# A trunk layer on one core: its SwiGLU products by Strassen's scheme, the down projection in a second pass

## The chip, the core and the metric

The kernel runs on one core of a Trainium2 chip. The core has a matrix engine (TensorE, PE in the profile), a vector engine (DVE), a scalar engine (ACT), GpSimd (POOL) and a sync engine (SP) whose queue issues the DMAs. Matrix products end in PSUM, eight banks of 512 float32 columns; everything else lies in SBUF or in DRAM. The metric is the device time of one execution in microseconds.

## The reference

One decoder layer over 1024 tokens of width 1024: three mixing branches, their gated merge, an output projection with residual, and a SwiGLU feed-forward part with its own residual. What matters here is the end:

```python
merged = sum_b sigmoid(gate_b) * (y_b @ w_branch[l, b])
x = x + merged @ w_out[l]
h2 = _rmsnorm(x, g_ffn[l])
x = x + (jax.nn.silu(h2 @ w_ffn_gate[l]) * (h2 @ w_ffn_up[l])) @ w_ffn_down[l]
```

`w_out` is 1024 x 1024, `w_ffn_gate` and `w_ffn_up` 1024 x 2816, `w_ffn_down` 2816 x 1024; all is float32.

## The kernel before

All dense products run transposed: the weights are the stationary operand (128 x 128), the activations [channel, token] the moving one, 512 tokens at a time. Each float32 operand is split into a high and a low part, and a product is three passes, hi\*hi, hi\*lo and lo\*hi, which `mm3` (L839) issues. So one 128 x 128 weight tile against 512 tokens is three matmuls. A split is a copy to `hi` on ACT and a subtraction to `lo` on DVE (`load_split`, L830, for weights that SP loads 512 KB at a time).

The program has four stages. The branches (0 to 793 us) and the merge (`merge_lane`, 793 to 924 us, which leaves the merged activations split in `mgh` and `mgl`) come first. Then the output projection (L889 to L908, 924 to 1014 us): eight strips of 128 output channels; each loads x and its strip of `wout`, runs 8 x 3 x 2 matmuls over both halves of the tokens, adds the result to x in `acc[j]` on DVE, splits it straight into `h2h`/`h2l` with the norm's gain, and lets ACT square it and POOL sum the squares.

The SwiGLU stage (1014 us to the end) takes the 22 strips of 128 hidden channels in blocks of 3, 3, 3, 3, 3, 2, 2, 1, 2 (`BLOCKS`). For one strip `up_lane` (L920) runs 48 gate and 48 up matmuls, all on operands that are resident in SBUF. The norm's row factor `rbc` is multiplied onto the products afterwards (L942, L944), so the first products wait for no factor. Then come the SiLU, the product of the two and its split into `ah`/`al`. `down_lane` (L949) lets a block's activations meet the same block's rows of `wfd`: eight output strips, two banks each, with one DVE addition onto `acc` per bank (L962). A planner (`Lanes`) puts the PE work of these lanes in an order by estimated times, so that one block's down products run beside the next block's up products; the framework's scheduler then orders the other engines' instructions.

Of the kernel before, what the change touches and what calls it, by code (L numbers as in the profile page):

```python
# [19 lines left out]
P = 128  # L20
S = 1024
# [7 lines left out]
BLOCKS = (3, 3, 3, 3, 3, 2, 2, 1, 2)  # L29
WARM = 7  # L30
# ns between a lane's work on the tensor engine and its next, which waits for the other engines
# [45 lines left out]
def trunk(tc, xT, memT, wT, wmkv, wmq0, wmq1, wgv, wfox, a2, par, cst, wbr, wout, wfg, wfu, wfd, outT):  # L77
# [26 lines left out]
    def rsqrt_(out, x, n, inv):  # L104
        """out = (x * inv + eps) ** -0.5 for a few columns"""
# [3 lines left out]
    def row_factors(ssqs, bank, rcol, rb, dg):  # L109
        """squares [d part, tokens], to be summed -> rcol [token, tile], rb [any partition, tokens]"""  # L110
# [16 lines left out]
    # ------------------------------------------------------------------ phase A: projections and branches  # L127
# [31 lines left out]
    def gate_lane(js):  # L159
        """branch gates, transposed; they go where the other lanes wait"""  # L160
# [29 lines left out]
    def strip_lane(src, evac):  # L190
        """one transposed strip of 128 columns"""
# [15 lines left out]
    def mem_group(src, evac):  # L207
        """token-major, 256 columns of both tiles of memory tokens; src [4][P][512]"""
# [15 lines left out]
    def group_lane(src, n, nm, evac, gate=None):  # L224
        """token-major: out[token, n] for nm tiles of tokens; src [4][P][2 * n]"""
# [14 lines left out]
    def split_evac(ps, g, hi, lo):  # L240
        """hi + lo = ps * g (g per partition)"""
# [3 lines left out]
    def head_norm(src, junk, ss):  # L245
        """sums of squares of the 128 columns of each head"""
# [3 lines left out]
    # ---- start: x and the memory tokens  # L250
# [795 lines left out]
```

## Time and profile before

| | |
|---|---|
| measured, median of 3 | 1742.22 us (1742.14 to 1742.38) |
| the profiled execution | 1741.5 us, its span from the first to the last instruction |
| PE busy | 1728.5 us, 99% of the span |
| DVE, ACT, POOL busy | 781.8, 503.4, 122.2 us |
| matmuls | 8807, of which 384 in the output projection and 3168 in the SwiGLU stage |
| granted TensorE clock | 1.00 of the 2.4 GHz level nearly throughout, mean 0.998 |

The profile records one execution. "Busy" is the time in which an engine ran instructions. The chain of waits follows the last instruction back, at each step to what released it. A timeline lists instructions by start; several of one kind in a row are merged as "x2". The profile gives no other time of its execution than the span; the measured median lies 0.7 us above it.

### The profile page before, as it was taken

To read this page: it belongs to the slowest core of one execution; us is meant where nothing else is said; L and a number is where in the kernel's file an instruction comes from. 1 tells how busy PE (TensorE), PEld (TensorE's weight loads), DVE (VectorE), ACT (ScalarE), POOL (GpSimd) and SP (SyncE) were. 2 spreads that over 40 slices of the span, in tenths; PEclk is the share of its full clock that TensorE was granted. 3 is DMA by queue.
4 is the path that set the end of the run, shared out by engine and by line. 5 is a ranking of instruction groups with operands and counts; after the bars stand their busy time and mean duration, and the time that the engine had idled before them with its cause. 6 is when DMAs were issued, how large, how long until landed. Compare 5 with 4: busy or idle time off the path is not lost.

```text
span 1741.5 us, 21268 instructions
## 1 busy us (share of the span) xinstructions
PE 1728.5 (99%) x8807; PEld 1467.4 (84%) x8807; DVE 781.8 (45%) x1268; ACT 503.4 (29%) x859; POOL 122.2 (7%) x94
## 2 busy tenths in 40 slices
PE   8999999999999999999999999999999999999999
PEld 6789988879789999988888878888888888888887
DVE  8435554352436555544474343333433343334435
ACT  6334553232224444433122232121211212121110
POOL 2000000000001000000352210000000000000000
PEclk9999999999999999999999999999999999999999
DMA  6341221111222121117653131110211111111002
GB/s 228 129 129 55 67 74 50 61 61 49 68 88 70 57 73 45 67 64 243 193 191 112 37 111 49 43 55 33 63 47 52 49 49 48 45 52 48 35 13 97
DMA packets 55985, 135.01 MB, mean 78 GB/s; under 512 B 5440, under 2 KB 20304, under 8 KB 55888
## 3 DMA queue, kind: packets, MB, share of 16 engines
q1 hardware_dynamic: 55888, 133.65, 23.5%
q8 instruction: 69, 1.13, 0.3%
q14 instruction: 28, 0.23, 0.0%
HBM read 110.49 MB, written 23.13 MB: 77 GB/s over the span
## 4 chain that ended last, share of the span: by engine, by line
PE 95%; DVE 2%; ACT 1%; DMA 1%; issue 0%; POOL 0%; SPq 0%; DVEq 0%
PE ps L841 18%; PE ps L843 18%; PE ps L845 18%; PE pt L155 5%; PE pt L156 4%; PE pt L157 4%; PE pm L234 4%; PE pm L236 4%; PE pm L235 4%; PE pm L197 2%; PE pm L201 2%; PE pm L199 2%; PE at L789 1%; PE o L801 1%; PE o L802 1%; PE at L762 0%
## 5 line engine op out<-in xcount | busy, mean ns | idle before, releaser
L841 PE MATMUL ps<-h2h,hi 128*128 128x512 f32 x704 | 217.2, 390 | 0.0
L843 PE MATMUL ps<-h2l,hi 128*128 128x512 f32 x704 | 216.9, 389 | 0.0
L845 PE MATMUL ps<-h2h,lo 128*128 128x512 f32 x704 | 216.8, 389 | 0.0
L835 ACT CAST hi<-raw 128x1024 fp32r<-128x1024 f32 x76 | 80.0, 1053 | 415.1 <-PE ps L843 383.7
L234 PE MATMUL pm<-whi,hh 128*128 128x384 f32 (+2 forms) x512 | 162.2, 317 | 0.0
L236 PE MATMUL pm<-whi,hl 128*128 128x384 f32 (+2 forms) x512 | 158.9, 310 | 0.0
L235 PE MATMUL pm<-wlo,hh 128*128 128x384 f32 (+2 forms) x512 | 158.8, 310 | 0.0
L845 PEld LDWEIGHTS ps<-h2h,lo 128*128 128x128 f32 x704 | 132.1, 188 | 27.9 <-DVE lo L836 0.4
L841 PEld LDWEIGHTS ps<-h2h,hi 128*128 128x128 f32 x704 | 132.1, 188 | 27.8 <-ACT hi L835 0.4
L843 PEld LDWEIGHTS ps<-h2l,hi 128*128 128x128 f32 x704 | 132.1, 188 | 27.6
L962 DVE TENSOR_TENSOR acc<-acc,ps 128x512 f32<-128x512 f32 x144 | 92.2, 684 | 120.0 <-PE ps L845 120.0
L155 PE MATMUL pt<-hh,whi 128*128 128x512 f32 x352 | 141.8, 403 | 0.0
L156 PE MATMUL pt<-hl,whi 128*128 128x512 f32 x352 | 137.8, 391 | 0.0
L157 PE MATMUL pt<-hh,wlo 128*128 128x512 f32 x352 | 137.7, 391 | 0.0
L843 PE MATMUL ps<-al,dh 128*128 128x512 f32 x352 | 108.7, 389 | 0.0
L841 PE MATMUL ps<-ah,dh 128*128 128x512 f32 x352 | 108.7, 389 | 0.0
L845 PE MATMUL ps<-ah,dl 128*128 128x512 f32 x352 | 108.7, 389 | 0.0
L836 DVE TENSOR_TENSOR lo<-raw,hi 128x1024 fp32r<-128x1024 f32 x76 | 99.0, 1304 | 18.7 <-ACT hi L835 18.4
L944 DVE TENSOR_TENSOR up<-ps,rbc 128x512 f32<-128x512 f32 x44 | 28.4, 686 | 166.5 <-PE ps L845 166.5
L234 PEld LDWEIGHTS pm<-whi,hh 128*128 128x128 f32 x512 | 96.3, 188 | 2.6
L235 PEld LDWEIGHTS pm<-wlo,hh 128*128 128x128 f32 x512 | 96.4, 188 | 2.5
L236 PEld LDWEIGHTS pm<-whi,hl 128*128 128x128 f32 x512 | 96.2, 188 | 0.0
(283 smaller groups left out, 2884.6 us busy)
## 6 DMA issues: line engine op xcount, KB each, us to landing
tg<-tg_d SPq DMA_DIRECT2D x24, 512.0 KB, 4.3
raw<-in_wT SPq DMA_DIRECT2D x22, 512.0 KB, 4.1
tg_d<-gz SPq DMA_DIRECT2D x22, 512.0 KB, 2.9
raw<-in_wfg SPq DMA_DIRECT2D x22, 512.0 KB, 3.5
raw<-in_wfd SPq DMA_DIRECT2D x22, 512.0 KB, 3.6
raw<-in_wfu SPq DMA_DIRECT2D x22, 512.0 KB, 3.5
raw<-in_wfox SPq DMA_DIRECT2D x16, 384.0 KB, 3.1
raw<-y_d SPq DMA_DIRECT2D x12, 512.0 KB, 4.6
```

The source lines that it names most:

```text
L155: nc.tensor.matmul(ps, hi[:, ks], hh[k][:, sl], start=k == 0, stop=False)
L156: nc.tensor.matmul(ps, hi[:, ks], hl[k][:, sl], start=False, stop=False)
L157: nc.tensor.matmul(ps, lo[:, ks], hh[k][:, sl], start=False, stop=k == KT - 1)
L234: nc.tensor.matmul(ps[:, :n], hh[k][:, ms], hi, start=k == 0, stop=False)
L235: nc.tensor.matmul(ps[:, :n], hh[k][:, ms], lo, start=False, stop=False)
L236: nc.tensor.matmul(ps[:, :n], hl[k][:, ms], hi, start=False, stop=k == KT - 1)
L835: nc.scalar.copy(hi, raw)
L836: nc.vector.tensor_tensor(lo, raw, hi.bitcast(F32), ALU.subtract)
L841: nc.tensor.matmul(ps, hi, a, start=first, stop=False)
L843: nc.tensor.matmul(ps, hi, b, start=False, stop=False)
L845: nc.tensor.matmul(ps, lo, a, start=False, stop=last)
L962: nc.vector.tensor_tensor(acc[j][:, s], acc[j][:, s], ps, ALU.add)
```

## The change

The SwiGLU products become Strassen products of the Winograd form. For a pair of hidden strips, the weights are a 2 x 2 block matrix (two strips by two halves of 512 channels) and the activations too (two halves of 512 channels by two halves of 512 tokens). Seven half-size products (`SEQ`) stand for eight. Four of the seven stationary operands are sums of weight blocks, which DVE computes for every pair (`weights`); four of the seven moving operands (T1 to T4) are sums of activation blocks. The sums of the products are formed in PSUM, by accumulating several products onto one of three banks `a`, `b`, `c`, and reading a bank out in between.

The down projection is done the same way, but its inner dimension is now eleven pairs, so it runs as a second pass: `gate_up(p)` writes the seven forms of the activations to `act_d[p]` in DRAM and the sums of the down weights to `sum_d[p]`; `down` takes them back in four blocks of 3, 3, 3 and 2 pairs (`DOWN`). The residual x waits in DRAM (`x_d`) meanwhile.

The output projection is run by halves of the tokens, so that the first half's norm factor is known early. The normed activations now carry their factor before they are split (`normed`, `hop`), instead of having it multiplied onto the products. Everything before the merge's end stays, but for the pool of the merge's weights, which now lies in a stack that is closed after the merge; the tiles of the later stages take its place.

```diff
-BLOCKS = (3, 3, 3, 3, 3, 2, 2, 1, 2)
+NP = NF // 2
+DOWN = (3, 3, 3, 2)
...
+    w4 = lambda: ws.tile([P, S], F32, tag="w4", bufs=5, name="w4")
+    h4 = lambda: ws.tile([P, S], F32R, tag="h4", bufs=3, name="h4")
+    l4 = lambda: ws.tile([P, S], F32R, tag="l4", bufs=3, name="l4")
...
+    def out_half(h):
...
+        for j in range(KT):
+            x1[j][h] = x = cell("x1")
+            nc.sync.dma_start(x, xT[j][:, sl])
+            raw = w4()
+            nc.sync.dma_start(raw, wout[j])
+            hi, lo = split(h4(), l4(), raw)
+            ps = bank8()
...
+            nc.vector.tensor_tensor(x, x, ps, ALU.add)
+            nc.sync.dma_start(x_d[j][h], x)
+            sq = ws.tile([P, 512], F32, tag="h2", bufs=2, name="sq") if j else ssq
+            nc.scalar.activation(sq, x, AF.Square)
+            if j:
+                nc.vector.tensor_tensor(ssq, ssq, sq, ALU.add)
+            yield ssq
...
+    SEQ = (("b", "A11", "B11"), ("a", "A12", "B21"), ("b", "S2", "T2"), ("c", "S1", "T1"), ("b", "S3", "T3"),
+           ("c", "S4", "B22"), ("b", "A22", "T4"))
+
+    def products(A, B, nk, reads):
+
+        banks = {}
+        for i, (bk, an, bn) in enumerate(SEQ):
+            first = bk not in banks
+            if first:
+                banks[bk] = bank8()
+            ps = banks[bk]
+            for k in range(nk):
+                (ah, al), (bh, bl) = A(an, k), B(bn, k)
+                mm3([ps], ah, al, [(bh, bl)], first and k == 0, k == nk - 1, not first)
+            reads[i](ps)
+            yield
...
+        def keep(t, i, l):
+            def read(ps):
+                t[i][l] = cell("t")
+                nc.scalar.copy(t[i][l], ps)
+            return read
+
+        def plus(t, i, l, then):
+            def read(ps):
+                add(t[i][l], ps, t[i][l])
+                then(i, l)
+            return read
...
+        reads = lambda t, then, last: [keep(t, 0, 0), plus(t, 0, 0, then), keep(t, 0, 1), keep(t, 1, 1),
+                                       plus(t, 1, 1, then), plus(t, 0, 1, then), last]
...
+        sub(t1, b12, b11)
+        sub(t2, b22, t1)
+        sub(t3, b22, b12)
+        sub(t4, b21, t2)
+        for i, t in enumerate((b11, b21, t2, t1, t3, b22, t4)):
+            nc.sync.dma_start(act_d[p][i], t)
+        a11, a12, a22, a21 = d = [cell("d") for i in range(4)]
+        for o in range(4):
+            nc.sync.dma_start(d[o].rearrange("p (j c) -> p j c", c=P), wfd[:, p, :, o, :].rearrange("j p c -> p j c"))
...
+    for k in range(4):
+        (b11, b12), (b21, b22) = x1[k], x1[k + 4]
+        normed(k, 1)
+        normed(k + 4, 1)
+        t2 = w4()[:, :512]
+        sub(b11, b12, b11)
+        sub(t2, b22, b11)
+        hops["T2", k] = hop(hp2, "hb", 20, t2)
+        sub(b21, b21, t2)
+    for k in range(4):
+        hops["T1", k] = hop(hp2, "hb", 20, x1[k][0])
...
+    def down(p0, n, last):
+        ops = {}
+        for i in range(0, 7, 2):
+            for q in range(n):
+                w = min(2, 7 - i)
+                raw = w4()
+                nc.sync.dma_start(raw[:, :w * 512].rearrange("p (o c) -> p o c", c=512),
+                                  act_d[p0 + q][i:i + w].rearrange("o p c -> p o c"))
+                for o in range(w):
+                    t = (hp1, "ha", 8) if i == 0 else (hp2, "hb", 20)
+                    ops[ORDER[i + o], q] = hop(*t, raw[:, o * 512:(o + 1) * 512])
...
+            def into(j, h, done):
+                def read(ps):
+                    t = acc[j][h]
+                    add(t, ps, t)
```

`cell` is a pool of 16 tiles of 128 x 512; it holds the merge's sums, then x, then all of `gate_up`'s results in turn, then `acc`.

Three places show how the instructions stand. The first is ACT where the merge ends. `mgh` is the high part of the merged activations, by strips; the copies to `hi` and to `h_8327` are the first splits of `wout`. Before:

```order
L835 CAST hi<-raw 128x1024
L882 ACTIVATE mgh_7326<-acc_7315 128x512 x2
L882 ACTIVATE mgh_7327<-acc_7316 128x512 x2
L835 CAST hi<-raw 128x1024
L882 ACTIVATE mgh_7328<-acc_7317 128x512 x2
```

and after:

```order
L885 ACTIVATE mgh_7334<-acc 128x512 x2
L885 ACTIVATE mgh_7335<-acc 128x512 x2
L885 ACTIVATE mgh_7336<-acc 128x512
L903 CAST h_8327<-w_8325 128x1024
L885 ACTIVATE mgh_7336<-acc 128x512
L903 CAST h_8363<-w_8361 128x1024
```

The first strip's split stood three strips of the merge ahead; it now stands behind the first half of the last one. Its load waits for one of the merge's last three matmuls, since its tile lies where the merge's weights lay.

The second place is DVE where the output projection ends and the SwiGLU stage begins. Before, with the last two strips' additions and splits of x (`acc`, `h2l`), then the down weights' low part `dl` and the factor (`rc`, `diag`):

```order
L903 TENSOR_TENSOR acc_7316<-acc_7316,ps 128x512 x2
L836 TENSOR_TENSOR lo<-raw,hi 128x1024
L243 SCALAR_TENSOR_TENSOR h2l_8286<-acc_7316,pr,h2h_8278 128x512 x2
L903 TENSOR_TENSOR acc_7317<-acc_7317,ps 128x512 x2
L243 SCALAR_TENSOR_TENSOR h2l_8287<-acc_7317,pr,h2h_8279 128x512 x2
L935 TENSOR_TENSOR dl<-raw,dh 128x1024 x2
L106 TENSOR_SCALAR rc_8815<-ps 128x8
```

After, the last of a row of 30 instructions that stand between the second half's factor and the first operand of T1 (`x_8791`, `x_8473` and so on are blocks of x, `w_9098` and the like the sums T2, `hbl` the low parts):

```order
L995 TENSOR_TENSOR x_8791<-x_8943,x_8791 128x512
L995 TENSOR_TENSOR x_8473<-x_8473,w_9098 128x512
L904 TENSOR_TENSOR hbl<-w_9098,hbh 128x512
L995 TENSOR_TENSOR x_8511<-x_8511,w_9108 128x512
L904 TENSOR_TENSOR hbl<-w_9108,hbh 128x512
L995 TENSOR_TENSOR x_8549<-x_8549,w_9118 128x512
L904 TENSOR_TENSOR hbl<-w_9118,hbh 128x512
L995 TENSOR_TENSOR x_8587<-x_8587,w_9128 128x512
L904 TENSOR_TENSOR hbl<-w_9128,hbh 128x512
L904 TENSOR_TENSOR hbl<-x_8323,hbh 128x512
```

The 30 are 8 normed multiplications, 16 subtractions, one split of weights and five low parts. PE's S2\*T2 of the first gate pair accumulates onto bank `b`, which ACT must first copy out; the copy goes into the cell of `x_8323`, so it waits for the last row shown.

The third place is DVE where the first pass ends and the second begins. Before, down products of one block stood among the up work of the next:

```order
L962 TENSOR_TENSOR acc_7315<-acc_7315,ps 128x512 x2
L962 TENSOR_TENSOR acc_7316<-acc_7316,ps 128x512 x2
L935 TENSOR_TENSOR dl<-raw,dh 128x1024 x2
L962 TENSOR_TENSOR acc_7317<-acc_7317,ps 128x512 x2
L935 TENSOR_TENSOR dl<-raw,dh 128x1024
```

After, from the last product of the last pair (L1050) to the first addition of the down projection:

```order
L1050 TENSOR_TENSOR t<-ps,t 128x512
L904 TENSOR_TENSOR l_12373<-w_12359,h_12372 128x768
L995 TENSOR_TENSOR T<-t 128x512
L904 TENSOR_TENSOR l_12377<-w_12360,h_12376 128x768
L904 TENSOR_TENSOR l_12383<-w_12380,h_12382 128x384
L995 TENSOR_TENSOR T<-t,T 128x512
L995 TENSOR_TENSOR T<-t 128x512
L904 TENSOR_TENSOR l_12478<-w_12467,h_12477 128x768
L995 TENSOR_TENSOR T<-t,T 128x512
L904 TENSOR_TENSOR l_12492<-w_12489,h_12491 128x384
L994 TENSOR_TENSOR d<-d 128x512
L994 TENSOR_TENSOR acc<-ps,acc 128x512
```

The third product of the first down group needs that addition, since it uses the same bank. `d` are the last pair's down weights, whose loads stand on SP behind the writes of the T tiles above, and the loads of `acc` stand behind those.

## Rows read from the trace of the kernel before

**Rows 1.** The page: busy time by engine (part 1), the chain that ended last (part 4).

```profile
PE 1728.5 (99%) x8807; PEld 1467.4 (84%) x8807; DVE 781.8 (45%) x1268; ACT 503.4 (29%) x859; POOL 122.2 (7%) x94
...
PE 95%; DVE 2%; ACT 1%; DMA 1%; issue 0%; POOL 0%; SPq 0%; DVEq 0%
```

**Rows 2.** Busy time by window: us, instructions, granted clock (PEclk), DMA share, GB/s.

```profile
20.00:25.00 5.00, 4.60 (x13) 3.65 (x14) 5.00 (x4) 2.37 (x4) 2.47 (x1) 0.66 0.65 240
885.00:920.00 35.00, 35.00 (x156) 29.01 (x155) 26.36 (x29) 10.76 (x15) 18.60 (x13) 1.00 0.71 227
924.00:1014.00 90.00, 90.00 (x388) 72.14 (x387) 31.90 (x41) 24.05 (x30) 20.84 (x8) 1.00 0.18 59
1200.00:1300.00 100.00, 100.00 (x443) 82.77 (x442) 36.61 (x51) 16.59 (x21) 0.00 (x0) 1.00 0.15 48
```

**Rows 3.** Timeline of PE in the last strip: start, duration, instruction.

```profile
1734.99 0.39 PE L843 MATMUL ps<-al,dh 128*128 128x512 f32 x1
...
1737.26 0.39 PE L845 MATMUL ps<-ah,dl 128*128 128x512 f32 x1
```

**Rows 4.** Timeline of PE at the end of the output projection.

```profile
1012.36 0.63 PE L845 MATMUL ps<-mgh,lo 128*128 128x512 f32 x2
...
1013.76 0.63 PE L845 MATMUL ps<-mgh,lo 128*128 128x512 f32 x2
```

**Rows 5.** Groups by line and shape, 900 to 1741 us: busy us, mean ns, idle before.

```profile
L835 ACT CAST hi<-raw 128x1024 fp32r<-128x1024 f32 x52 | 54.8, 1054 | 342.0 <-PE ps L843 333.2 <-DMA raw<-in_wfg 5.7 <-DMA raw<-in_wfu 2.9
...
L947 DVE TENSOR_TENSOR al<-up,ah 128x512 fp32r<-128x512 f32 x44 | 28.5, 688 | 1.8
...
L946 ACT CAST ah<-up 128x512 fp32r<-128x512 f32 x44 | 26.9, 622 | 67.5 <-DVE up L945 67.5
...
L123 PE MATMUL ps<-diag,ones 128*128 128x512 f32 x4 | 2.0, 618 | 0.6 <-DVE diag L118 0.6
L114 PE MATMUL ps<-ones,ssq 128*128 128x1 f32 x16 | 1.9, 251 | 0.0
...
L943 ACT ACT_TABLE_LOAD x1 | 1.3, 1283 | 0.0
```

**Rows 6.** Timeline of DVE in the output projection.

```profile
1002.99 1.28 DVE L903 TENSOR_TENSOR acc<-acc,ps 128x512 f32<-128x512 f32 x2 [7.46 <-PE ps L845]
1004.19 1.22 DVE L836 TENSOR_TENSOR lo<-raw,hi 128x1024 fp32r<-128x1024 f32 x1
1005.33 1.41 DVE L243 SCALAR_TENSOR_TENSOR h2l<-acc,pr,h2h 128x512 fp32r<-128x512 f32 x2
```

**Rows 7.** DMA issues: KB each, median us to landing.

```profile
raw<-in_wout SPq DMA_DIRECT2D x8, 512.0 KB, 3.5
...
raw<-in_wgv SPq DMA_DIRECT2D x8, 256.0 KB, 2.7
...
y_d<-y SPq DMA_DIRECT2D x32, 128.0 KB, 2.9
```

**Rows 8.** Timeline where the merge ends: wait and its releaser in brackets.

```profile
913.53 1.05 ACT L835 CAST hi<-raw 128x1024 fp32r<-128x1024 f32 x1 [1.02 <-PE ps L843]
...
924.17 0.61 PE L845 MATMUL ps<-hi,lo 128*128 128x512 f32 x2
...
924.62 0.63 PE L841 MATMUL ps<-mgh,hi 128*128 128x512 f32 x2
...
928.96 0.63 ACT L882 ACTIVATE mgh<-acc 128x512 fp32r<-128x512 f32 x1 [1.59 <-POOL acc L880]
```

**Rows 9.** Timeline of PE around an early idle time.

```profile
20.40 0.50 PE L156 MATMUL pt<-hl,w 128*128 128x512 f32 x1 [2.03 <-DVE hl L243]
...
24.09 0.45 PE L156 MATMUL pm<-hl,w 128*128 128x512 f32 x1
```

More of the change, by code (lines that the diff above doesn't have):

```diff
@@ L854, in trunk @@
     ap_ = pool(root, "acc")
-    acc = [ap_.tile([P, S], F32, name=f"acc{k}") for k in range(KT)]
+    cell = lambda name: ap_.tile([P, 512], F32, tag="cell", bufs=16, name=name)
+    acc = [[cell("acc") for h in range(2)] for k in range(KT)]
     BM = ExitStack()
@@ L966, in ffn_lane @@
-    def ffn_lane():
-        lanes.add(factor_lane(), 0)
-        yield lambda: 0 if pools else None
-        f = 0
-        for b, nb in enumerate(BLOCKS):
-            dw, act = [], []
-            for i in range(nb):
-                yield from up_lane(pools[0], f, dw, act)
-                f += 1
-            lanes.add(down_lane(b, dw, act), 0 if b < len(BLOCKS) - 2 else 2 + b)
-    BM.close()
-    pools = [pool(root, "ffn")]
-    lanes.add(ffn_lane(), 1)
-    lanes.run()
+    ws = pool(root, "wstage2", side="right")
@@ new lines, in half_factors @@
+    def half_factors(h, ssq):
+        rcol = cp.tile([P, 4], F32, tag="rcol", bufs=2, name="rcol")
+        dg = ws.tile([P, 512], F32, tag="h2", bufs=2, name="dg")
+        ps = bank8()
+        for t in range(4):
+            nc.tensor.matmul(ps[:, t:t + 1], ssq[:, t * P:(t + 1) * P], ones[:, 0:1], start=True, stop=True)
+        rsqrt_(rcol, ps[:, :4], 4, 1.0 / D)
+        nc.vector.tensor_tensor(dg.rearrange("p (t c) -> p t c", c=P), ident.unsqueeze(1).broadcast_to([P, 4, P]),
+                                rcol.unsqueeze(2).broadcast_to([P, 4, P]), ALU.mult)
+        yield
+        ps = bank8()
+        nc.tensor.matmul(ps, ones, dg, start=True, stop=True)
+        nc.scalar.copy(rbc[:, H2[h]], ps)
+        yield
@@ new lines, in normed, with hop @@
+    def normed(k, h):
+        x = x1[k][h]
+        nc.vector.scalar_tensor_tensor(x, x, pr[:, C_GFFN + k:C_GFFN + k + 1], rbc[:, H2[h]], ALU.mult, ALU.mult)
+        return x
+    def hop(pl, tag, n, src):
+        return split(pl.tile([P, 512], F32R, tag=tag + "h", bufs=n, name=tag + "h"),
+                     pl.tile([P, 512], F32R, tag=tag + "l", bufs=n, name=tag + "l"), src)
+    halves = [out_half(h) for h in range(2)]
+    for ssq in halves[0]:
+        pass
+    fac = half_factors(0, ssq)
@@ new lines, in trunk @@
+    for j, ssq in enumerate(halves[1]):
+        if j in (0, 1):
+            next(fac)
+        if j == 1:
+            for k in range(KT):
+                hops["B11" if k < 4 else "B21", k % 4] = hop(hp1, "ha", 8, normed(k, 0))
+    fac = half_factors(1, ssq)
+    SEQ = (("b", "A11", "B11"), ("a", "A12", "B21"), ("b", "S2", "T2"), ("c", "S1", "T1"), ("b", "S3", "T3"),
[11 more added lines that the diff above has]
+            reads[i](ps)
+            yield
@@ new lines, in trunk @@
+    run = gate_up(0)
+    next(run)
+    next(fac)
+    next(run)
+    next(run)
+    next(fac)
+    for k in range(4):
[9 more added lines that the diff above has]
+        hops["T1", k] = hop(hp2, "hb", 20, x1[k][0])
+    for k in range(4):
+        sub(x1[k][1], x1[k + 4][1], x1[k][1])
+        hops["T3", k] = hop(hp2, "hb", 20, x1[k][1])
@@ L982, in trunk @@
+    p0 = 0
+    for n in DOWN:
+        down(p0, n, p0 + n == NP)
+        p0 += n
     pe.__exit__(None, None, None)
```

217 lines of the change are left out of this document (134 added, 83 removed).

## The prediction

> **What bounds the kernel now.** I read the page's busy times first: PE is busy for 1728.5 of 1741.5 us, and the chain that ended last lies on PE for 95% [rows 1]. So the time is the number of matmuls times their pitch, and any idle time of PE adds to it. Next the windows: in the SwiGLU stage 443 matmuls start per 100 us, 0.226 us each, at a granted clock of 1.00, while DVE is busy for 37% and ACT for 17% of the time and the DMA engines for 15% [rows 2]. All engines but PE have room. Last the timelines, for what one matmul costs in each form: ten matmuls that follow one another on one bank in the last strip take 2.27 us, 0.227 each [rows 3], as the new products will run; pairs on two banks in the output projection are slower, six in 1.40 us, 0.233 each [rows 4].
>
> **Part 1, fewer matmuls.** Before, the SwiGLU stage has 22 strips x 96 = 2112 gate and up matmuls and 22 x 48 = 1056 down, 3168 in all. After, a pair has 2 x 7 products of 4 tiles x 3 passes, 168, and 11 pairs 1848; down has 4 groups x 7 products x 11 pairs x 3 passes = 924; together 2772. The output projection keeps 384. The 396 that go are worth 396 x 0.2265 = **-89.7 us**, all of it on the path. The factor's small products stay the same in sum. The new operands could run at the slower pitch of [rows 4]: 2772 x 0.007 = +19 us; if the output projection, now on one bank, went at 0.2265, that is 384 x 0.007 = -3 us. I take 0 for both, since the one-bank chain of [rows 3] is the nearest row; the ends stay for the range.
>
> **Part 2, the merge's end.** Now PE passes from merge to output projection without a gap, at 924.62, since the first strip was split at 913.53 [rows 8]. In the new order its load waits for one of the merge's last three matmuls, so is issued at about 924.2. It lands after 3.5 us or more [rows 7]; then comes the copy, 1.05 [rows 8], then the low part, 1.22 [rows 6], which on DVE stands behind nothing late. That is 930 at the earliest, and 931.5 with five loads in flight beside it. The last merged strip's high part, at 928.96 plus 0.63 [rows 8], would not be later. PE does two matmuls in between: an idle time of 5 to 7 us, 6.3 taken. After an idle time of 2.03 us PE ran slower until 24.09 [rows 9]: the window of 20 to 25 us has a mean granted clock of 0.66 [rows 2], so (1 - 0.66) / 0.5 x 5 = 3.4 us at the level of 1.2 GHz, which cost 1.7 us. I add 1.7 to each stall longer than that. **+8 us**, 5 to 10.
>
> **Part 3, from the output projection into the first gate pair.** This is the largest price. Before, the first product waited for no factor. Now T0 is the end of the last strip. PE can run four products whose operands stem from the first half of the tokens, 4 x 12 x 0.2265 = 10.9 us. Between them stand the factor's products: for the whole of the tokens they take 1.9 + 2.0 us [rows 5], so half of that, 1.95; and u's first split, which on DVE stands behind the last strip's square sum, costs PE some 1.75. PE is through at T0 + 14.6. The factor itself comes by this order: g's first product 2.7, the sums 0.95, g's second product 2.7, the late split 1.75, u's first product 2.7, the broadcast product 1.0, then on ACT a split's copy and the row's copy, 0.6 each [rows 5]: T0 + 13. Only then can DVE run the 30 instructions up to the first operand of T1: 8 normed multiplications at 0.705, 16 subtractions and 5 low parts at 0.64, one split at 1.22 [rows 6], 20.3 us. PE's S2\*T2 waits for ACT's copy of bank b, that copy for the cell which the last of the 30 frees: T0 + 34. So PE idles 1.75 + 19.4, and 1.7 more for the clock. Next, DVE has 17 more instructions before it reads bank b after S3\*T3, then additions, a wait for the first SiLU with its table load of 1.28 [rows 5], and a split: about T0 + 51, while PE would be there at T0 + 46.7 (four products and 1.7 us of slow clock after 34.1); 4.3 and 1.7 again. Sum **+29 us**. If the 30 go at the single durations of 0.69 [rows 5], it is 31; with the late part hidden 22. Range 22 to 35.
>
> **Part 4, ten steady pairs.** One pair is 168 x 0.2265 = 38.1 us of PE. DVE has per pair six splits at 1.22 and 28 instructions (sums, additions, products, two short splits) at 0.64, 25 us, 66%; ACT some 13; the DMAs 5.75 MB, 151 GB/s. The nearest row is that of the merge, 885 to 920 us: 227 GB/s at a share of 0.71, and PE busy throughout [rows 2]. A bank is read under one product of 2.72 us; the read costs 0.64 and what stands before it on its engine, at most a split of 1.22 or a copy of 1.05. That fits; for a lapse now and then I take 0.4 us a pair, **+4 us**, 0 to 10.
>
> **Part 5, from the first pass to the second.** The third product of the first down group needs an addition that on DVE stands behind eleven instructions: 0.64 for the last product, five splits (three of 0.95, two of 0.55, by width from 1.22) and four T sums and one sum of down weights at 0.64. On SP the T writes, the d loads and the loads of `acc` follow one another. By the DVE row alone the addition would end 8.5 us after the last up product; with the last d load, which can only be issued when T4 is there at 7 us and lands 2.7 to 3 us later [rows 7], at about 12. PE has two products, 4.1 us, to run. **+9.5 us** with the clock's 1.7; 5 to 13.
>
> **Part 6, the second pass.** Four blocks take 3 x 57 + 38 us of PE. For three pairs DVE has 21 low parts (13.4) and 4 x 7.7 to 8.1 = 31.6 us of splits and additions, 45 of 57 us; DMAs 10.6 MB, 190 GB/s. Within a group a bank must be read under one product of 2.04 us: addition 0.64 behind a split of 0.95 fits, and with two pairs, 1.36 us against 0.64 + 0.64, barely. At the three block changes the next block's low parts fall on the last group: 13 low parts, 7 additions and a split are 13.8 us of DVE in 14.3 of PE, while their loads pass five buffers and the next weights' load comes last. I take 3 us for each of these, clock included for some, and 2 for the small waits: **+11 us**, 3 to 25.
>
> The sum: -89.7 + 8 + 29 + 4 + 9.5 + 11 = -28 us against the profiled span of 1741.5, 1713.3; the median lies 0.7 above the span: **1714 us**. All ends at their low side give -55, at their high side +3 without the pitch.
>
> A page of the Trainium skill bears on the 1.7 us: "TensorE: Matmul & The Clock Gate", sections on why this matters for kernels and on the second failure mode, says that idle gaps between bursts of matmuls put the array on the lower clock, and that many small gaps between groups, from cycling through PSUM banks, can do so as well. By the first, the seams cost the lower clock too, as [rows 9] shows; without it the sum would be some 7 us lower. No run here shows the second yet; what it would do is in the last rival.
>
> **Rivals.** (a) The seams cost less: parts 4 to 6 nearly nothing, since DVE is idle for a third of both passes, and part 3 at its low end. -89.7 + 8 + 22 + 3 = -57: 1686 us. For it: DVE has 33% and 21% in hand. Against: the waits are an order on one queue, not load.
> (b) The second pass loses at its block changes what the high end says (25) and the new operands run at part of the slower pitch, +8: 1714 + 14 + 8 = 1736 us. For it: DVE is at 97% around a change; [rows 4] shows that pitch is not one number.
> (c) It becomes slower: the second pass is bound by bank reads. A group returns to bank b after one product, and if in each of the 16 groups one read comes so late that PE idles 2 us and the clock falls, a group costs 2 + 1.7: 59 us in place of 11, 1762 us. It decides from 43 us in the second pass (11 + 28 + 4) on. For it: additions stand behind splits that wait for loads, and every load passes five buffers. Against: within a group DVE is at 57% of PE's time. (The second rule of that page is this mechanism.)
> (d) The change does not do what it says: the seven products need as many matmuls. The count above speaks against it; I give it nothing.
>
> **Chances.** Forecast case, 1700 to 1727: 0.53; (a), below 1700: 0.14; (b), 1727 to 1738.7: 0.14; within 3.5 us of before, about what a measurement of this kernel can tell: 0.05; (c), above 1745.7: 0.14. The range leaves out (c) and the lower part of (a), some 0.05: 1692 to 1745 us. Faster by over 0.2% 0.81, within 0.05, slower 0.14.
>
> **What would show it.** Some 396 matmuls fewer in the count, pitch 0.226 in both passes. Four idle stretches of PE: 6 us at 925, 20 us some 14 us after the output projection's end, and a second of 4 there, 8 us where the down part begins; each followed by a window below 1.00. In the second pass the releaser of PE's waits should be DVE's additions at block changes only. The forecast is wrong if the steady pairs take over 39 us, or a down group of three pairs over 15 us.

## The result, and the profile after

The changed kernel takes 1756.04 us, median of runs from 1754.24 to 1757.78, against 1742.30 us for the kernel before, measured beside it: a ratio of 1.0078, with a 95% interval of 1.0064 to 1.0092. It is slower, and the time lies outside the predicted range of 1692 to 1745 us. The profiled execution has a span of 1754.6 us, 13.1 us longer than the span before.

The page of the changed kernel, first the busy times by engine, then the chain that ended last (as [rows 1] of before):

```profile
PE 1665.9 (95%) x8411; PEld 1393.1 (79%) x8411; DVE 989.3 (56%) x1577; ACT 628.9 (36%) x1072; POOL 103.1 (6%) x88
...
PE 75%; DVE 9%; DMA 9%; SPq 3%; issue 2%; ACT 2%; POOL 0%; DVEq 0%; ACTq 0%
```

The 396 matmuls are gone (8411 instructions of PE instead of 8807), and PE is busy for 62.6 us less. Yet the span is longer, so PE, idle for 13 us before, now stands idle for 88.7 us. The chain says the same: it lies on PE for 75% of the span instead of 95%, and on DVE and the DMAs for 9% each.

The waits of PE after, summed by what it waited for (us in total, times, longest in us):

```profile
PE ps L843 <- ACT t L1031: 35.2, 11, 21.3
PE ps L843 <- DVE acc L994: 21.6, 9, 14.1
PE ps L843 <- DVE t L994: 8.9, 10, 1.6
PE ps L843 <- ACT h L903: 8.4, 3, 6.8
```

The first row is the first long wait for ACT, 21.3 us in the first gate pair, plus ten waits of 1.39 us, one in each pair that follows. The second is the seam between the two passes, 14.1 us, and the small waits of the second pass. The third is DVE, about once a pair. The fourth is mostly the end of the merge.

Four stretches of the changed kernel (busy us and instructions of PE, PEld, DVE, ACT and POOL, then granted clock, DMA share, GB/s):

```profile
924.00:940.00 16.00, 9.43 (x28) 7.03 (x29) 6.59 (x8) 5.02 (x6) 2.48 (x2) 0.68 0.85 312
1030.00:1080.00 50.00, 27.32 (x104) 20.77 (x103) 39.35 (x60) 22.23 (x36) 0.79 (x1) 0.76 0.14 47
1100.00:1200.00 100.00, 95.07 (x406) 75.57 (x405) 59.96 (x82) 31.96 (x46) 0.00 (x0) 1.00 0.48 151
1500.00:1600.00 100.00, 82.23 (x343) 64.63 (x342) 67.40 (x101) 35.36 (x55) 0.00 (x0) 0.93 0.77 245
```

The third row is the steady state, and answers to the last of [rows 2]: PE is busy for 95.07 us in 100 and starts 406 matmuls instead of 443, at a granted clock of 1.00. DVE at 60% and ACT at 32% are far from full. The other three rows hold the merge's end, the first gate pair and the seam; from the merge's end on, the clock falls there alone.

Where the 13.1 us come from, by the prediction's parts. Each length is taken from the start of one stage's first matmul to the next, against the count of matmuls at 0.2265 us:

| part | forecast, us | measured, us | how measured |
|---|---|---|---|
| 1 fewer matmuls | -89.7 | -89.7 | 396 x 0.2265 |
| 1 pitch of the new operands | 0 (up to 19) | +14.4 | 2772 matmuls at 0.2317 on the average |
| 2 merge's end | +8 | +8.8 | merge ends 1.0 earlier; PE idle 6.95; 2.9 more in the output projection |
| 3 first gate pair | +29 | +25.9 | 66.8 us against 38.05 + 1.95, less 0.9 of pitch |
| 4 ten steady pairs | +4 | +28.1 | 41.73 us each (41.48 to 42.43) against 38.05, less 8.7 of pitch |
| 5 first down group | +9.5 | +15.9 | 30.5 us against 14.27, less 0.3 of pitch |
| 6 rest of the second pass | +11 | +11.7 | 211.2 us against 195.0, less 4.5 of pitch |

The sum is +15.1 us. The 2 us too many are in the base: the SwiGLU stage of before took 723.3 us, not the 721.5 that 3168 matmuls and the factor's products make.

**The pitch.** The timeline of PE in a steady pair (start, duration, instruction):

```profile
1136.15 0.39 PE L843 MATMUL ps<-hah,h 128*128 128x512 f32 x1
...
1138.64 0.39 PE L847 MATMUL ps<-hah,l 128*128 128x512 f32 x1
...
1142.63 0.40 PE L843 MATMUL ps<-hbh,h 128*128 128x512 f32 x1
...
1146.83 0.40 PE L843 MATMUL ps<-hbh,h 128*128 128x512 f32 x1
```

The first two rows are eleven matmuls apart, on the operands `ha`: 2.49 us, 0.226 each. The last two are eighteen apart, on the operands `hb` (the sums T1 to T4 and B22): 4.20 us, 0.233 each. All of them run on one bank at a time. So the slower pitch of [rows 4] is back, and five of a pair's seven products have it.

**The steady pair.** The timeline of ACT, DVE and PE in the same pair:

```profile
1138.84 1.04 ACT L903 CAST h<-w 128x1024 fp32r<-128x1024 f32 x1 [4.85 <-PE ps L845]
...
1139.79 0.58 ACT L1031 COPY t<-ps 128x512 f32<-128x512 f32 x1
...
1140.43 0.50 PE L843 MATMUL ps<-hbh,h 128*128 128x512 f32 x1 [1.40 <-ACT t L1031]
...
1146.80 0.69 DVE L994 TENSOR_TENSOR d<-d 128x512 f32<-128x512 f32 x1 [3.73 <-DMA d<-in_wfd]
...
1151.80 1.28 DVE L994 TENSOR_TENSOR t<-ps,t 128x512 f32<-128x512 f32 x2
...
1152.54 0.50 PE L843 MATMUL ps<-hbh,h 128*128 128x512 f32 x1 [0.64 <-DVE t L994]
```

At 1138.64 PE starts the last matmul ahead of the third product, which goes onto bank `b`, so ACT must copy that bank out first. The copy (L1031) stands on ACT behind a cast of the next weights (L903), and the cast waits for the buffer that PE is still reading. PE resumes at 1140.43: 1.56 us more than the pitch. Later DVE stands still for 3.73 us, until the last pair's down weights `d` have landed. The addition that reads bank `b` after S3\*T3 (L994, `t<-ps,t`) is queued behind that and behind what then follows. PE was through with that product at about 1149 and has run S4\*B22 in between; the read starts only at 1151.80, and A22\*T4, which goes onto bank `b` again, at 1152.54, 0.8 us late.

**The seam.** The timeline of ACT, DVE, SP and PE where the down projection begins:

```profile
1514.98 0.51 ACT L903 CAST h<-w 128x384 fp32r<-128x384 f32 x1 [1.94 <-DMA w<-in_wfd]
1515.53 0.56 DVE L904 TENSOR_TENSOR l<-w,h 128x384 fp32r<-128x384 f32 x1 [1.50 <-ACT h L903]
...
1518.08 0.69 DVE L995 TENSOR_TENSOR T<-t,T 128x512 f32<-128x512 f32 x1
...
1519.92 0.57 SPq L1073 DMA_DIRECT2D act_d<-T  x1
1520.54 0.46 SPq L1076 DMA_DIRECT2D d<-in_wfd  x1
1521.04 2.92 SPq L1136 DMA_DIRECT2D acc<-x_d  x5
...
1526.22 0.69 DVE L994 TENSOR_TENSOR d<-d 128x512 f32<-128x512 f32 x1 [4.98 <-DMA d<-in_wfd]
1526.83 0.69 DVE L994 TENSOR_TENSOR acc<-ps,acc 128x512 f32<-128x512 f32 x1
...
1527.67 0.76 PE L843 MATMUL ps<-hbh,h 128*128 128x512 f32 x1 [14.14 <-DVE acc L994]
```

The last up product ends, and the down projection begins, at 1509.06. The four loads of `d` alternate on SP with the writes of the T tiles. The T sums stand on DVE among splits of the second pass's weights, and one of these waits for a cast that waits for its load (1.94 and 1.50 us). So the last sum, T4, starts only at 1518.08, and the last `d` is issued at 1520.54, 11.5 us after the pass's begin. DVE's first addition on these loads comes at 1526.22, after 4.98 us of idle time, and the read of the bank stands behind it. How long such transfers took (KB each, median us from issue to landing):

```profile
act_d<-T SPq DMA_DIRECT2D x44, 256.0 KB, 6.0
d<-in_wfd SPq DMA_DIRECT2D x44, 256.0 KB, 6.2
```

A load of `d` takes 6.2 us beside the writes of T, not the 2.7 to 3 us of [rows 7].

**The first gate pair and the merge's end.** PE's last matmul before the long gap, and the first after each gap:

```profile
930.52 0.79 PE L843 MATMUL ps<-mgh,h 128*128 128x512 f32 x1 [6.79 <-ACT h L903]
...
1039.75 0.39 PE L847 MATMUL ps<-hah,l 128*128 128x512 f32 x1
...
1061.39 0.79 PE L843 MATMUL ps<-hbh,h 128*128 128x512 f32 x1 [21.25 <-ACT t L1031]
```

The first product of the output projection starts at 930.52, S2\*T2 of the first pair at 1061.39, which is 36.4 us after that stage's begin at 1024.95. ACT and DVE ahead of that second start:

```profile
1052.45 8.41 ACT L903 CAST hbh<-x 128x512 fp32r<-128x512 f32 x16
...
1057.23 4.89 DVE L904 TENSOR_TENSOR hbl<-x,hbh 128x512 fp32r<-128x512 f32 x8
...
1060.76 1.05 ACT L1031 COPY t<-ps 128x512 f32<-128x512 f32 x2
```

The first of the eight DVE instructions is the last of the 30 in the section on the change; it frees the copy's cell at about 1057.9. The copy of bank `b` starts 2.9 us later: it stands on ACT behind 16 casts that follow one another without a gap. So it waited for ACT's own queue in the end, and not for that row of DVE.

### The profile page after: what moved, and what is told of

Its sections match the earlier page's. It is cut to its first block, busy times and chain, and to the rows that moved or that the text cites. A ratio compares the mean times of both kernels' runs of the same rounds, so it can differ in the third digit from the quotient of the medians.

```text
span 1754.6 us, 21924 instructions
## 1 busy us (share of the span) xinstructions
PE 1665.9 (95%) x8411; PEld 1393.1 (79%) x8411; DVE 989.3 (56%) x1577; ACT 628.9 (36%) x1072; POOL 103.1 (6%) x88
## 4 chain that ended last, share of the span: by engine, by line
PE 75%; DVE 9%; DMA 9%; SPq 3%; issue 2%; ACT 2%; POOL 0%; DVEq 0%; ACTq 0%
PE ps L843 11%; PE ps L845 11%; PE ps L847 11%; PE pt L156 4%; PE pt L158 4%; PE pt L157 4%; PE pm L235 4%; PE pm L236 4%; PE pm L237 4%; DMA d<-in_wfd 4%; PE pm L198 2%; DMA w<-act_d 2%; DVE l L904 2%; PE pm L202 2%; PE pm L200 2%
## 5 line engine op out<-in xcount | busy, mean ns | idle before, releaser
L843 PE MATMUL ps<-hbh,h 128*128 128x512 f32 x660 | 265.7, 403 | 66.3 <-ACT t L1031 35.2
L903 ACT CAST h<-w 128x1024 fp32r<-128x1024 f32 (+4 forms) x168 | 144.6, 861 | 368.5 <-PE ps L845 296.6
L845 PE MATMUL ps<-hbl,h 128*128 128x512 f32 x660 | 262.4, 398 | 0.0
L847 PE MATMUL ps<-hbh,l 128*128 128x512 f32 x660 | 262.3, 397 | 0.0
L904 DVE TENSOR_TENSOR l<-w,h 128x1024 fp32r<-128x1024 f32 (+4 forms) x168 | 166.0, 989 | 92.5 <-ACT h L903 92.4
L843 PEld LDWEIGHTS ps<-hbh,h 128*128 128x128 f32 x660 | 124.9, 189 | 108.3 <-ACT t L1031 39.8
L847 PEld LDWEIGHTS ps<-hbh,l 128*128 128x128 f32 x660 | 124.8, 189 | 30.3
L845 PEld LDWEIGHTS ps<-hbl,h 128*128 128x128 f32 x660 | 125.0, 189 | 28.6
L994 DVE TENSOR_TENSOR acc<-ps,acc 128x512 f32<-128x512 f32 x112 | 76.8, 689 | 50.3 <-PE ps L847 47.6
L843 PE MATMUL ps<-hah,h 128*128 128x512 f32 x264 | 103.7, 393 | 0.9 <-ACT h L903 0.9
L847 PE MATMUL ps<-hah,l 128*128 128x512 f32 x264 | 103.2, 391 | 0.9 <-DVE l L904 0.8
```

The costliest lines, as they stand in the source:

```text
L843: nc.tensor.matmul(ps, hi, a, start=first, stop=False, skip_group_check=more)
L845: nc.tensor.matmul(ps, hi, b, start=False, stop=False, skip_group_check=more)
L847: nc.tensor.matmul(ps, lo, a, start=False, stop=last, skip_group_check=more)
L903: nc.scalar.copy(hi, raw)
L904: nc.vector.tensor_tensor(lo, raw, hi.bitcast(F32), ALU.subtract)
L994: add = lambda o, a, b: nc.vector.tensor_tensor(o, a, b, ALU.add)
```

## The experiments

The theory after reading the two traces: the loss of the steady pairs has three causes, the pitch, set by where the two operands lie in SBUF; the order on ACT, a cast ahead of a copy; and the order on DVE, an addition that waits for a load ahead of a bank read. The rivals: the pitch comes from the region of memory that an operand lies in; the waits are one chain, so that taking one away only moves it; DVE's load is what counts, so that work must leave it.

All times below are medians beside runs of the kernel before on the same chip (1741.5 to 1742.3 us). "Pair" is the mean of the ten steady pairs in the one run that was profiled; that run lay 4.6 us above the median in e3 and 3.8 above it in e10, so their pairs are a little too long.

| experiment | us | ratio to before | 95% interval | pair, us |
|---|---|---|---|---|
| after | 1756.04 | 1.0078 | 1.0064 to 1.0092 | 41.73 |
| e2_pad | 1746.51 | 1.0025 | 1.0015 to 1.0034 | 41.44 |
| e3_keep_first | 1750.71 | 1.0044 | 1.0030 to 1.0058 | 41.67 |
| e4_rows | 1746.35 | 1.0029 | 1.0019 to 1.0038 | 41.20 |
| e5_keep_rows | 1741.46 | 0.9999 | 0.9990 to 1.0008 | 40.44 |
| e6_three | 1735.64 | 0.9964 | 0.9950 to 0.9977 | 40.20 |
| e7_four | 1716.35 | 0.9853 | 0.9836 to 0.9869 | 38.57 |
| e8_before_shift | 1738.76 | 0.9985 | 0.9975 to 0.9994 | |
| e9_sums_early | 1729.54 | 0.9931 | 0.9916 to 0.9946 | 39.68 |
| e10_four_pieces | 1720.48 | 0.9876 | 0.9860 to 0.9893 | 39.26 |
| e11_four_unshifted | 1726.05 | 0.9913 | 0.9898 to 0.9927 | 39.28 |
| e12_five | 1719.77 | 0.9878 | 0.9863 to 0.9892 | 38.48 |

### The pitch by itself: e1_probe

Behind the end, ten rows of 24 equal matmuls, each row with its operands at other places; nothing reads their results, and they make the time 50 us longer.

`H` and `Lw` are the two parts of a tile of weights, `b1` and `b2` are `hb` tiles; `hs(t, o)` and `mv(t, o)` begin `o` columns of 4 bytes into a tile.

```diff
...
+    for stat, mov in ((hs(H, 0), mv(Lw, 0)), (hs(H, 0), mv(Lw, 8)), (hs(H, 0), mv(Lw, 16)), (hs(H, 0), mv(Lw, 24)),
+                      (hs(H, 0), mv(Lw, 32)), (hs(H, 0), mv(Lw, 56)), (hs(b1[0], 0), mv(b2[0], 0)),
+                      (hs(b1[0], 0), mv(Lw, 0)), (hs(H, 0), mv(b2[0], 0)), (hs(H, 56), mv(b2[0], 0))):
+        ps = bank8()
+        for i in range(24):
+            nc.tensor.matmul(ps, stat, mov, start=i == 0, stop=i == 23)
```

> The changed kernel with ten rows of 24 matmuls behind its end, 128x512 each on one bank, that nothing reads; the rest is computed as before. It measures the pitch by where the two operands lie. Known from the changed kernel: moving tiles ha (byte 143328 and up of a partition) with weights at 200672 and up run at 0.227 us, moving tiles hb (57536 to 139456) with the same weights at 0.233. Theory A, alignment: what counts is whether both addresses have the same remainder by 512 bytes (weights 480, ha 480, hb 192). Then both operands in the upper tiles at offset 0 take 0.227, with the moving one shifted by 32, 64, 96, 128 or 224 bytes some or all 0.233; weights from hb with moving hb 0.227; weights from hb with moving upper tile 0.233; weights upper with moving hb 0.233; the same with the weights shifted by 224 bytes, so that the remainders agree, 0.227. Theory B, region: upper with upper 0.227 at every shift, hb with hb 0.227, mixed 0.233 with or without a shift.

The timeline of PE in the probe; a row's start less the one before, by 24, is the pitch:

```profile
1781.16 5.61 PE L1186 MATMUL ps<-hbh 128*128 128x512 f32 x24
1786.61 5.77 PE L1186 MATMUL ps<-l,hbh 128*128 128x512 f32 x24
1792.21 5.76 PE L1186 MATMUL ps<-hbh,h 128*128 128x512 f32 x24
1797.80 5.62 PE L1186 MATMUL ps<-hbh,h 128*128 128x512 f32 x24
```

The row at 1781.16 has weights and moving operand both among the `hb` tiles: 5.45 us, 0.227 each. The row at 1786.61 has its weights there and its moving operand among the weights' tiles: 5.60 us, 0.233 each. The last two rows have their weights in H and their moving operand in `hb`, the second of them with the weights 224 bytes further. Means from the first to the last start within each of the ten rows:

| weights | moving operand | pitch, us |
|---|---|---|
| H | Lw, same remainder by 512 bytes | 0.228 |
| H | Lw, 32, 64, 96 bytes further | 0.233, 0.229, 0.234 |
| H | Lw, 128, 224 bytes further | 0.233, 0.233 |
| `hb` | `hb` | 0.227 |
| `hb` | Lw | 0.233 |
| H | `hb` | 0.233 |
| H, 224 bytes further (the remainder of `hb`) | `hb` | 0.228 |

The last two rows decide: the same two tiles, and a shift of the weights by 224 bytes brings the pitch back. It isn't the region, nor the kind of product; it is the distance of the two start addresses. That it counts by 512 bytes fits all rows and the kernel, whose weight blocks start 512 bytes apart and run at one pitch on `ha`; a distance of 256 was not tried, so the period may be 256 as well. The tiles `h4`, `l4` and `ha` lie at remainder 480, `hb` at 192.

### The pitch in the kernel: e2_pad and e8_before_shift

A tile of 288 bytes that nothing uses shifts the later tiles, so that `hb` and the merged activations come to the weights' remainder; in the kernel before, one of 320 bytes does it for the merged activations.

```diff
+    pool(root, "pad").tile([P, 72], F32, name="pad")
     ap_ = pool(root, "acc")
```

> The changed kernel with 288 bytes left free ahead of the cells, so that mgh, mgl and the hb tiles have the same remainder by 512 bytes as the weights. Theory A: the products on hb, 5 of 7 in both passes, 1980 matmuls, and the 384 of the output projection go from 0.233 to 0.227: 2364 x 0.0065 = 15 us less than the changed kernel, about 1741 us. Theory B: no change, 1756 us.

> The kernel before with 320 bytes left free ahead of acc, so that mgh and mgl have the same remainder by 512 bytes as the weights of the output projection. If the remainder is what makes the pitch of 0.233, its 384 matmuls go at 0.227: 384 x 0.0065 = 2.5 us less than before, with all other stages alike. Rival: nothing changes.

In e2 the pitch is 0.227 in the output projection, in the pairs and in the second pass. But the time falls by 9.5 us, less than the pitch gives back (14.4 us, and 2.2 in the output projection). PE's waits in e2:

```profile
PE ps L843 <- ACT t L1032: 35.2, 11, 21.3
...
PE ps L843 <- DVE t L995: 13.7, 9, 2.3
```

The wait for DVE in the pairs, 8.9 us in the changed kernel, is 13.7 now; I read that as a faster PE that comes to the same late read earlier. In e8 the kernel before gains 2.7 us, about 384 x 0.007, and its output projection takes 87.0 us instead of 89.6: the slower pitch of [rows 4] was there from the start.

### One order at a time: e3_keep_first, e4_rows and e9_sums_early

e3 holds the cast of the next weights back behind the copy that the third product needs. For that the up weights' loads and splits also stand earlier in the program, behind the first gate product instead of the last:

```diff
-    def split(hi, lo, raw):
-        nc.scalar.copy(hi, raw)
+    def split(hi, lo, raw, behind=None):
+        cast = nc.scalar.copy(hi, raw)
+        if behind is not None:
+            tc.add_manual_dep(cast.ins, behind.ins.name, ...)
...
+            yield from (next(gg_) for i in range(1))
+        wu = weights(wfu[p], kept[-1] if p else None)
```

> The changed kernel with one edge of order on ACT: the copy of bank b after a gate product stands ahead of the cast of the next weights, which waits for the second product to free its buffer. Theory: the copy behind that cast is the 1.4 to 1.6 us by which PE waits at S2*T2 in each gate half; gone, 10 pairs give 14 to 16 us, about 1741 us. Rival: another wait ends last there (DVE's low part or its addition), and less than 4 us is gained.

```profile
PE ps L843 <- DVE t L999: 21.7, 10, 2.7
PE ps L843 <- ACT t L1036: 21.3, 1, 21.3
```

These are PE's waits in e3. Of the wait for ACT the first pair's 21.3 us alone are left, so the cast was its cause. But the wait for DVE has grown from 8.9 to 21.7 us, and the time fell by 5.3 us only, where I had expected 14 to 16. Whether PE's earlier arrival or the earlier place of the up weights' work on DVE made that wait grow was not tried apart.

e4 loads `d` from an input laid out so that each partition reads one piece of 2 KB instead of four of 512 bytes:

```diff
-            nc.sync.dma_start(d[o].rearrange("p (j c) -> p j c", c=P), wfd[:, p, :, o, :].rearrange("j p c -> p j c"))
+            nc.sync.dma_start(d[o], wfe[p, o])
```

> The changed kernel with the down weights of the first pass read in 2 KB rows (a second copy of them in DRAM, laid out so) in place of 512-byte pieces. Theory: their landing in 6.2 us is what DVE's queue waits for, 46 us in all, and behind it the addition for which PE waits before the last product of a half (0.6 to 1.5 us, ten times), and the same loads hold up the start of the second pass. Then landing falls to some 3 us, the ten waits vanish (-9 us) and the start of the second pass comes 3 us earlier: about 1744 us. Rival: the waits stem from the number of DVE instructions in that place, and only the 3 us are gained, 1753 us.

```profile
PE ps L843 <- ACT t L1031: 35.2, 11, 21.3
...
PE ps L843 <- DVE t L994: 3.2, 6, 1.5
```

PE's waits in e4: the wait for DVE fell from 8.9 to 3.2 us, that for ACT stayed. The time fell by 9.7 us, 5.3 of it in the ten pairs. The landing in some 3 us that I had expected did not come: the median load still took 6.2 us. Yet DVE's first addition on `d` starts some 0.6 us earlier in most pairs, 12.9 us after the pair's begin instead of 13.5, and its wait for `d` in all is shorter, 39.4 us instead of 46.3. That was enough for the small waits of PE.

e9 leaves the loads as they are, but issues them, with the sums of `d` and their writes, ahead of the up products instead of behind the T tiles:

```diff
+        if p:
+            downs()
         yield from uu_
...
-        a11, a12, a22, a21 = d = [cell("d") for i in range(4)]
...
+        if p == 0:
+            downs()
```

> The changed kernel with one edit: the down weights' sums of a pair are formed in the middle of the pair, so their loads no longer wait for the pair's last write and DVE's first addition on them no longer stands ahead of the bank reads of the next gate half. Theory C: DVE's wait at the last product of the gate half goes (10 x 1.1), ACT's of 1.5 stays, a pair takes 40.6 in place of 41.7; the start of the second pass gains 5: together 16 us less than the changed kernel, 1740 us. Rival: the chain is not set by these loads; less than 6 us.

PE's waits in e9, and DVE's wait for `d` in the changed kernel and in e9:

```profile
PE ps L843 <- ACT t L1031: 22.7, 2, 21.3
...
PE ps L843 <- DVE t L994: 2.9, 3, 1.4
```

```profile
DVE d L994 <- DMA d<-in_wfd: 46.3, 11, 6.7
...
DVE d L994 <- DMA d<-in_wfd: 57.4, 11, 7.7
```

The one edit takes 26.5 us off, where I had expected 16, and the kernel is faster than the one before. DVE still stands idle for `d`, 57.4 us in all and longer than the 46.3 us of the changed kernel; but now no bank read that is due soon stands behind it, so PE waits 2.9 us instead of 8.9. The wait for ACT went as well, to 22.7 us, without an edit of ACT: the order that results has the copy ahead of the cast. The first down group took 26.9 us instead of 30.5, since the last pair's `d` no longer stands between the T tiles and `acc`.

### Together: e5_keep_rows, e6_three, e7_four, e10_four_pieces, e11_four_unshifted

e5 has the edits of e3 and e4, e6 the shift of e2 as well, and e7 all four. e10 is e7 with the loads of `d` in four pieces, e11 is e7 without the shift. Their diffs are the ones above.

> The edge on ACT and the loads in 2 KB rows together. Theory C, two waits in turn: in a steady pair PE is held either at S2*T2 by ACT's copy or at the last product of the gate half by DVE's addition, whose place is set by the end of the pair before (T sums, their write, the loads of the down weights behind it on SP); so each edit alone moved most of its gain into the other wait. Together they give more than the 6 and 8.5 us that each gave alone: 41.7 us a pair become 39 to 39.5, some 24 us less than the changed kernel, about 1728 to 1732 us. Rival: they add up, 14 to 15 us, 1741 us.

> The same two edits and the 288 bytes that bring all operands to the same remainder by 512 bytes. Theory C: a pair comes down to 38.1 plus 0.5, the second pass and the output projection gain 5 and 2.5 us: about 1719 us. Rival: another chain sets a pair's length at 40 or more, 1730 us or above.

> The same three edits, and the down weights' sums of a pair are formed in the middle of the pair instead of after it, so that their loads do not stand ahead of the loads of acc at the start of the second pass. Theory: PE's wait of 12 to 14 us in the first down group shrinks to about 5, what eleven DVE instructions cost beyond two products: 8 us less than with three edits. Rival: the loads of acc still stand behind the writes of the last T tiles and take as long, 1 us less.

> The kernel with four edits, but with the 512-byte pieces again. If the place of the loads in the queues was the cause and their length only made it worse, a pair stays below 39.5 us and the time within 5 us of the four edits, 1716 to 1721 us. Rival: the pieces themselves hold the queue, a pair takes 40 or more, 1730 us.

> The kernel with four edits, but without the 288 bytes. In the changed kernel the shift gave 9 us, since steady pairs filled up with waits. Where those waits are gone the pitch must show in full: 10 x 120 + 660 products on hb in the second pass and 384 in the output projection, 2250 x 0.0065 = 14.6 us more than with the shift, 1731 us. Rival: 5 us, hidden as before.

e5 gained 14.6 us, about the sum of the two edits alone (5.3 + 9.7): I had expected 24, and the rival, that they merely add, was right. e6 came to 1735.64, not 1719: with the pitch and the order on ACT mended and the loads in rows, PE still waited 16.5 us for DVE in the pairs. Only with the loads moved did these waits nearly go: e7 is 19.3 us faster than e6, where I had expected 8. PE's waits in e7:

```profile
PE ps L843 <- ACT t L1037: 21.3, 1, 21.3
...
PE ps L843 <- DVE t L1000: 2.9, 3, 1.7
```

A pair takes 38.57 us, 0.5 above its matmuls. e7 is the fastest kernel of all, 25 us below the one before. Its span is 40.5 us below the changed kernel's: 31.6 in the pairs, 5.2 in the second pass, 3.0 in the output projection, 1.6 in the first pair, 1.2 in the gap ahead of the output projection, less 2.1 since its merge ends later. Both parts taken out of e7 count: the pieces cost 4.1 us (e10), the missing shift 9.7 us (e11), where 14.6 was to come if all of the pitch counted, and 5 if other waits took its place: it lies between. Beside e9, e11 is only 3.5 us faster: with the loads moved, the edits of e3 and e4 together are worth little more than what the pieces cost.

### The first gate pair: e12_five

What is left in e7 is mainly the 21.3 us in the first pair, where DVE runs the 30 instructions and ACT the 16 casts. e12 is e7 with eight of the subtractions on GpSimd, where nothing else runs then.

```diff
-        sub(b21, b21, t2)
+        nc.gpsimd.tensor_tensor(b21, b21, t2, ALU.subtract)
...
-        sub(x1[k][1], x1[k + 4][1], x1[k][1])
+        nc.gpsimd.tensor_tensor(x1[k][1], x1[k + 4][1], x1[k][1], ALU.subtract)
```

> The kernel with four edits, and the eight subtractions for T3 and T4 of the normed activations on GpSimd. They stood among the 30 DVE instructions ahead of PE's third product of the first pair. Theory: PE's idle time of 21.4 us there is that row of instructions; without eight of 0.64 it is 16.3, and the time 1711 us. Rival: with GpSimd at work DVE's own instructions slow down (before, a split took 1.99 in place of 1.22 us beside GpSimd's additions), or ACT's casts set the pace: less than 2 us.

The theory fell: 1719.77 us, slower than e7, and the first pair took 74.5 us instead of 65.2. The timeline of GpSimd in e12:

```profile
1042.69 15.70 POOL L1118 TENSOR_TENSOR x<-x,x 128x512 f32<-128x512 f32 x4 [14.07 <-DVE x L1001]
1058.36 5.84 POOL L1114 TENSOR_TENSOR x<-x,w 128x512 f32<-128x512 f32 x4
```

Four subtractions take 15.70 us, 3.9 each, so the casts that need them come one by one, and ACT's copy of bank `b` stands behind them. PE waits for it 25.0 us, and 3.6 us once more later in the pair. The load left DVE, and the wait grew. The trace of the changed kernel speaks for half of the rival too: ACT's casts already set the last 2.9 us of that wait there.

## Why the prediction was wrong

**Part 1.** The count was right, the pitch wrong. I had both numbers, 0.227 in [rows 3] and 0.233 in [rows 4], and put the difference down to one bank or two. The probe shows that the operands' addresses set it, and the output projection proves it too: now on one bank, it still runs at 0.233. Of the 19 us named as the end for this, 14.4 were paid; but the range up to 1745 us was added up without them, so the end stood in neither the sum nor the range. A price that two rows of one trace put differently, without a reason that they show, belongs in both.

**Part 2** was right in mechanism: 8.8 us against 8. The idle time was 6.95 us, within the 5 to 7, and the clock stayed at the lower level until 936.7, which cost some 3 us and not 1.7. That the sum met so well is partly luck: the merge, whose work no edit changes, ended 1.0 us earlier than before, and in the traces of the changed kernels it ends anywhere from 923.2 to 925.7.

**Part 3** was right in place and about in size: 25.9 against 29. S2\*T2 started 36.4 us after the stage's begin, where I had 34. DVE's 30 instructions were through after 33.0 us, where I had counted 33.3; the rest was ACT's row of casts ahead of the copy, which the prediction did not have. The idle time was 21.4 us instead of 19.4; the second one, of 4.3 us, did not occur.

**Part 4** is the step that failed: 28.1 us against 4, besides the pitch. I compared loads, 66% of DVE, and held one product of 2.72 us against the read and one instruction ahead of it. That does fit, as e7 shows with almost the same instructions in another order at 38.57 us a pair. But I checked only how long the instruction ahead of the read takes, not what that instruction waits for. On ACT it was a cast that waits for PE itself (10 x 1.56 = 15.6 us; gone in e3), on DVE an addition that waits for a load of 6.2 us, issued among the writes of the pair before (8.9 us by the waits, 10.5 with the 0.16 by which the lost time exceeds a wait; 3.2 us of waits left in e4). I had used just this reasoning in part 5, and not seen that the same instructions stand in each pair.

**Part 5** had the right mechanism and place, and the wrong price: 15.9 against 9.5. Two terms were too small. I had the last load of `d` issued 7 us after the last up product, and it was issued after 11.5: the T sums ahead of it waited on DVE for splits whose weights had not landed, where I had counted DVE's instructions alone. And I had it land in 2.7 to 3 us by [rows 7]; DVE started on it 5.7 us after the issue.

**Part 6** was right: 11.7 against 11, with a loss where I had it, at the changes of block: the first group of the second and third block took 17.5 and 17.6 us, against 14.6 of most others. The third group of each of the first three blocks, at 16 us, I did not have.

**The rivals.** The sign of (c) came true, but not its place: it put the late bank reads into the second pass, and they cost their time in the first. (b) had the pitch, at 8 instead of 14.4. The steady pairs have two waits each, which cost 0.8 and 1.6 us, and the window of 1100 to 1200 us has a granted clock of 1.00. The page "TensorE: Matmul & The Clock Gate" of the Trainium skill says in its section on the second failure mode that many small gaps between groups, from cycling through PSUM banks, can bring the clock down; that did not show here. After the long gaps the first matmuls ran at the lower level (0.43 us apart from 1061.39 to 1066, by the granted clock 1.2 GHz), which cost 1 to 3 us each time. That agrees with the same page of the Trainium skill, section on why this matters for kernels, on idle gaps between bursts.

The tests that I had named worked: pairs above 39 us and a first down group far above 15 us were to show the forecast wrong, and they did (41.73 and 30.5). What stays open: why e9's order also cured ACT was read from the order and the waits, and not tried alone; the first pair's 21 us were not removed by anything tried, and about 2 of the 28.1 us of part 4 lie in no wait that was named.

## What to carry to other kernels

Before trusting that a queue has room, list for each bank read what stands ahead of it on its engine and what each of those waits for: a DMA that lands late or a buffer that PE itself still holds is worth more than any share of busy time. Taking one wait away can feed the next one (e3: 13.9 us of waits for ACT gone, 12.8 us more for DVE), and mending both need not give more than the sum (e5); moving the wait to where nothing due stands behind it (e9) was worth more than making it shorter (e4). And when an edit moves tiles in SBUF, compare the start addresses of the two operands of each product before taking over a pitch.

## What the runs showed of the hardware

- These float32 matmuls of 128x512 run at 0.227 to 0.228 us when the weights and the moving operand start at the same remainder by 512 bytes, and at 0.229 to 0.234 us at the other distances tried, at a granted clock of 1.00. That is 1 to 3%. Why, the runs don't show.
- A GpSimd subtraction of 128x512 took 3.9 us in one stretch and 1.5 us in the next. The windows of these two stretches in e12 (the third pair of numbers is DVE):

```profile
1042.69:1058.36 15.67, 0.00 (x0) 0.00 (x0) 13.59 (x19) 6.36 (x11) 15.67 (x5) 0.50 0.00 0
1058.36:1064.20 5.84, 1.27 (x3) 1.08 (x4) 2.11 (x2) 5.42 (x10) 5.83 (x5) 0.50 0.42 126
```

  While DVE was busy for 13.59 of 15.67 us, four took 15.7 us; with DVE busy for 2.11 of 5.84 us, four took 5.8. The Trainium skill, page "SBUF — State Buffer", section on the two separate sides of SBUF, says that a DVE operation with two SBUF inputs and a GpSimd operation that reads SBUF exclude each other. This trace agrees for GpSimd, which loses 2.4 us each; DVE's own subtractions did not get longer in e12; in the kernel before, a DVE split of 128x1024 beside GpSimd's additions took 1.99 us instead of 1.22.
- A load of 256 KB in pieces of 512 bytes and one in rows of 2 KB landed after the same 6.2 us in the median (after and e4), and after 5.5 (pieces, e10) and 5.0 us (rows, e7) where they are issued elsewhere. In time, the place in the program (26.5 us, e9) counted more than the pieces (9.7 us in e4, 4.1 in e10).
